# Reordering the first products of a decoder layer, moving one accumulator to other PSUM banks, and giving one chain its own planner clock

## The chip, the cores and the metric

The kernel runs on one core of a Trainium2 chip (trn2). A core has a matrix engine (PE; its weight loads are listed apart as PEld), a vector engine (DVE), an activation engine (ACT), GpSimd (POOL) and a sync engine (SP, which issues most DMAs here). The metric is the device time of one execution in microseconds, the median over several runs. One execution was also taken by the hardware profiler; all rows below are from that one.

## The reference, cut to what matters

Two layers (DEPTH = 2) of a decoder trunk over a sequence of 256 rows of width 1024. In each layer one projection `z = h @ w_in` is split into the inputs of two mixers; their outputs are merged and projected, and an MLP and a gated embedding follow.

```
h = rmsnorm(x, norm_mix[i]);  z = h @ w_in[i]
(q_a, kc, vc, ks_, vs_, kw, vw, g_nsa, rq, rk, rv, rg, merge_a, merge_b) = split_cols(z, IN_SPLITS)
y_a = nsa_mixer(q_a, kc, vc, ks_, vs_, kw, vw, ...) @ w_up_nsa[i]
y_b = retention(rq, rk, rv, rg) @ w_up_ret[i]
mix = sigmoid(merge_a) * y_a + sigmoid(merge_b) * y_b
x = x + mix @ w_out[i]
x = x + square(relu(rmsnorm(x, norm_mlp[i]) @ w_ff1[i])) @ w_ff2[i]
x = x + sigmoid(rmsnorm(x, norm_ple[i]) @ w_ple_gate[i]) * (p[i] @ w_ple[i])
```

In the first mixer the keys and values `kc`, `vc` are cut into overlapping windows of 32 rows, passed through a small MLP (`gelu(zb @ w1) @ w2`) and give 16 compressed keys and values per group; queries attend to those, to the selected blocks and to a sliding window. With 256 rows all blocks are selected.

## The kernel before

**Tiles.** Every matrix product is made from two halves of each operand: `hi`, a copy rounded to the fast matmul type (ACT), and `lo`, the rest (DVE). A product is three matmuls, hi·hi, hi·lo, lo·hi (`three`, L214 records all matmuls). The activations are kept transposed in `XT`, 8 chunks of 128 x 256; their halves, scaled by the norm's gain, are `XH` and `XL` (`feed_x`). The factor of the norm itself comes later: `feed_sq` squares the chunks, `finish_a` sums the squares with one matmul over `ones` and raises to the power -1/2 on POOL (`r`), `finish_b` turns `r` into a row of 256 (`RB`).

**Weights** come in units of 512 KB (128 x 1024; kvg: 280 KB). `PLAN` lists the units in the order in which PE takes them. `unit_load` issues a unit's DMA on SP into one of 4 `raw` buffers, `unit_split` makes `hi` and `lo` into 6 buffers each, `take` hands them to PE, and `advance` keeps the splits 4 units ahead of PE. The first-layer MLP of the compressed keys (`w1`, named w0 to w7) has raw buffers of its own.

**The order on PE** is written out by hand: `ORDER` (L56) for the products from `w_in`, as far as rg3, and `_plan` (L70) for the rest. A kcvc, ksvs, rq or ff1 unit is 24 matmuls of 256 columns, a q, rv or rg unit 12 of 512 columns, a kvg unit 12 of 280, a w unit 4 of 512. `fa` and `fb` call `finish_a` and `finish_b`. `unit` (L863) accumulates q, kvg, ksvs, rv and rg in two banks of the PSUM pool `mm`, which has three; the pool `sc` has two banks and serves the attention's scores, and `ot` one.

**Work beside it.** `windows` (L880) runs when kcvc is complete and `fb` is done: DVE multiplies by `RB` (zt), adds the positions (zs) and splits (ZB), and ZB is what w0 to w7 multiply. `q_tail`, `kv_tail`, `compress`, `attend` (softmax) and `collect` (weigh, retain) are generators: each piece issues its PE, ACT and DVE instructions and yields a time at which the next may come. The planner keeps a virtual clock `vt["pe"]` that each matmul moves on, and books ACT, DVE and POOL work into the free stretches of those engines (`charge`, L157). `poke`, called between groups of matmuls, runs the pieces that are due; so the place of a piece in PE's queue is fixed when the program is built. A tile framework then orders ACT's and DVE's instructions; `tc.high_priority()` moves some ahead.

**At the end of attention**, `weigh` writes NHh and NHl, which the units ua0 to ua3 multiply; among these stand the matmuls (`ot<-rV,rs`) and the transposes of `retain`, whose RHh and RHl the units ub0 to ub3 multiply. In the MLP, `ff1(i)` makes one of 16 groups of 256 hidden columns from two units of four chunks each.

Of the kernel before, what the change touches and what calls it, by code (L numbers as in the profile page):

```python
# [15 lines left out]
P = 128  # L16
S = 256
# [28 lines left out]
for _n, _w in PAR_PARTS:  # L46
# [7 lines left out]


ORDER = (  # L56
# [4 lines left out]
)  # L61


def _seq(s):
    return [(x, 0) if x in ("fa", "fb") else (x[:-1], int(x[-1])) for x in s.split()]


SEQ = [_seq(s) for s in ORDER]


def _plan(l):
    r = [({"w": "w1"}.get(n, n), u) for n, u in SEQ[l] if n not in ("fa", "fb")]
    for n in ("ma", "mb"):
        r += [(n, u) for u in range(8)]
    r += [("ua", u) for u in range(4)] + [("ub", 0), ("ub", 1), ("ub", 2), ("out", 0), ("out", 1)]
    r += [("ub", 3)] + [("out", u) for u in range(2, 8)]
    r += [("ff1", u) for u in range(4)]
    for i in range(14):
        r += [("ff1", 2 * i + 4), ("ff1", 2 * i + 5), ("ff2", 2 * i), ("ff2", 2 * i + 1)]
    r += [("ff2", u) for u in range(28, 32)]  # L80
    r += [("ple", u) for u in range(2)]
    r += [("gate", u) for u in (0, 2, 4, 1, 3, 5, 6, 7)]
    return [(l,) + x for x in r]
# [11 lines left out]
def trunk(ctx: ExitStack, tc: tile.TileContext, xT, wu, wg, cst, msk, par, pin, out):  # L95
# [25 lines left out]
    def mm_tile(shape):  # L121
        return ps.tile(shape, F32, tag="mm", name=nm("mm"), bufs=3)
# [31 lines left out]

    gaps = {e: [[0.0, 1e9]] for e in ("act", "dve", "pool")}

    def charge(eng, us):  # L157
        us += 0.03
        gs = gaps[eng]
        while len(gs) > 1 and gs[0][1] < vt["pe"] - 6.0:  # L160
            gs.pop(0)
        for i, (a, e) in enumerate(gs):
            s = max(a, cur[0])
            if s + us <= e:
                new = []
# [99 lines left out]
    def load_x(a, b_):  # L265
        nc.sync.dma_start(XT[:, a:b_, :], xT[:, a:b_, :])
# [73 lines left out]
    def begin(st):  # L340

        while state["load"] < RAW:
            unit_load(state["load"])
            state["load"] += 1
            if state["load"] in (2, 3):
                load_x(2 * state["load"], 2 * state["load"] + 2)
        unit_split(0, lambda c: feed_x(st, c, 1))
        state["split"] = 1
        split_to(2 - AHEAD)
        for c in range(4, 8):  # L350
            feed_x(st, c, 1)
# [15 lines left out]
    bg = []  # L367
    LB = 7.0
    SL = 0.0
    DE = 1.0  # L370
    SLACK = {"kv_tail": 4.0, "q_tail": 3.0, "compress": 1.5, "attend": 1.0, "collect": 0.0}

    def spawn(gen, paced=False):
        bg.append([vt["pe"], gen, paced])
# [1 line left out]
    def step(gen):  # L376
        fresh()
        if gen.__name__ == "compress":
            with tc.high_priority():
                d = next(gen)  # L380
        else:
            d = next(gen)
        if d == "now":
            return cur[0]
        return (cur[0] if d is None else d) + SLACK.get(gen.__name__, SL)

# [45 lines left out]
    def feed_sq(st, c0, n):  # L432
        sq = ztile([P, n, S])
        act(sq, XT[:, c0:c0 + n, :], AF.Square)
        if c0 == 0:
            st["sq"] = sq
        else:
            acc = st["sq"][:, 0:n]
            tt(out=acc, in0=acc, in1=sq, op=ALU.add)
        if c0 + n == 8:  # L440
            acc = st["sq"]
            tt(out=acc[:, 0], in0=acc[:, 0], in1=acc[:, 1], op=ALU.add)
# [69 lines left out]
    def layer(l, st):  # L512
# [349 lines left out]

        def unit(name, u, k0, nk, width, first, last):  # L863
            if first:
                acc[name] = [mm_tile([P, width]) for _ in range(2)]
            a_unit(acc[name], take(l, name, u), XH, XL, k0, nk, width, first, last)

        def w1_unit(u):
# [45 lines left out]
        for name, u in SEQ[l]:  # L914
            if name == "kcvc":
                b_unit(pkv, take(l, "kcvc", u), XH, XL, 4 * u, u == 0, u == 1)
                if u == 1:
                    ready("kcvc")
            elif name == "fa":
                finish_a(st)  # L920
                r = st["r"]
                rh = small([P, 2], "rh")
                ts(out=rh, in0=r, scalar1=0.5, scalar2=None, op0=ALU.mult)
                rr = small([P, 2], "rr")
                tt(out=rr, in0=r, in1=r, op=ALU.mult)
                ready("fa")
            elif name == "fb":
                finish_b(st)
                RB = st["RB"]
                stt(out=gk, in0=PAR(l, "qn"), scalar=float(DH) ** -0.5, in1=PAR(l, "kn"),  # L930
                    op0=ALU.mult, op1=ALU.mult)
                ready("fb")
            elif name == "kvg":
                unit("kvg", u, 2 * u, 2, 280, u == 0, u == 3)
                if u == 3:
                    ready("kvg")
            elif name == "q":
                unit("q", u, 2 * u, 2, 512, u == 0, u == 3)
                if u == 3:
                    for t in range(2):  # L940
                        spawn(q_tail(t, acc["q"][t]))
                    poke()
            elif name == "ksvs":
                unit("ksvs", u, 4 * u, 4, 256, u == 0, u == 1)
                if u == 1:
                    for t in range(2):
                        spawn(kv_tail(1, t, acc["ksvs"][t]))
                    poke()
            elif name == "w":
                w1_unit(u)  # L950
                if u == 7:
                    spawn(compress(acc["w"]))
                    poke()
                    spawn(attend(), True)
                    spawn(collect(), True)
            else:
                if name in ("rq", "rk"):
                    i, hp = ("rq", "rk").index(name), u // 2
                    if u % 2 == 0:
                        acc[name] = mm_tile([P, 2, S])  # L960
                    b_unit(acc[name], take(l, name, u), XH, XL, 4 * (u % 2), u % 2 == 0, u % 2 == 1)
                    if u % 2 == 1:
                        fresh()
                        rope(i, hp, acc[name])
                    continue
                unit(name, u, 2 * u, 2, 512, u == 0, u == 3)
                if u < 3:
                    continue
                for t in range(2):
                    pq = acc[name][t]  # L970
                    fresh()
                    if name == "rv":
                        act(rV[:, t, :], pq, AF.Copy, scale=rr[:, t:t + 1])
# [85 lines left out]
        act(ph, pT, AF.Copy)  # L1059
        sub(pl, pT, ph.bitcast(F32))  # L1060

        def ff1(i):
            pm = mm_tile([P, 2, S])
            for u in range(2):
                b_unit(pm, take(l, "ff1", 2 * i + u), XH, XL, 4 * u, u == 0, u == 1)
            au = big([P, 2, 2, S], f"B{i % 3}", "au")
            ho = big([P, 2, 2, S], f"B{3 + i % 4}", "ho", F32R)
            a, u2 = au[:, 0], au[:, 1]
            h, o = ho[:, 0], ho[:, 1]
            act(a, pm, AF.Relu)  # L1070
            tt(out=h, in0=a, in1=a, op=ALU.mult)
            act(u2, a, AF.Square)
            sub(o, u2, h.bitcast(F32))
            ff[i] = (h, o)
# [9 lines left out]
                for n in range(4):  # L1084
                    wide(pf[n], w, n, h[:, u, :], o[:, u, :], i == 0 and u == 0, False)

        ff1(0)
        ff1(1)
        finish_a(stf)
        ff1(2)  # L1090
        finish_b(stf, square=True)
# [206 lines left out]
```

## Time and profile before

| | us |
|---|---|
| median of 3 runs | 869.22 (869.02 to 869.53) |
| the profiled execution's own time | 870.81 |
| its span, from the first to the last instruction | 868.70 |
| PE busy | 848.6 (98% of the span) |
| DVE busy | 613.1 (71%) |
| ACT busy | 501.1 (58%) |
| DMA, mean | 175 GB/s |

Rows of the timeline have a start, a duration, the engine and line, what is written from what, and in brackets the idle time just before and what ended it. A matmul's duration is modelled and overlaps the next one's: 0.28 us is listed for one of 256 columns, while 48 of them take 5.70 us, 0.119 each. What a stretch costs on PE is therefore read from starts, and not from busy time.

### The profile page before, as it was taken

The page shows a single profiled execution, that of the slowest core. Times are in us where ns is not written, and L with a number is a line of the kernel's source. Part 1 is how long each engine was busy: PE and PEld are TensorE (multiplying, and loading weights), DVE is VectorE, ACT ScalarE, POOL GpSimd, SP SyncE. Part 2 cuts the span into 40 slices and gives each one's busy share as a digit, 9 for nine tenths or more (in the row PEclk, how much of TensorE's full clock was granted, in tenths as well). Part 3 has the DMA queues.
Part 4 walks back from the last instruction along what each step waited for, and adds up shares of the span by engine and source line. Part 5 has one row for each costly group of instructions (what it writes and reads, how often), then busy time and mean ns, then how long its engine had stood idle before and what let it go on. Part 6 is the DMA issues. An engine that isn't in the chain of part 4 may idle for free.

```text
span 868.7 us, 16475 instructions
## 1 busy us (share of the span) xinstructions
PE 848.6 (98%) x6647; PEld 817.3 (94%) x6647; DVE 613.1 (71%) x1011; ACT 501.1 (58%) x836; POOL 38.9 (4%) x32
## 2 busy tenths in 40 slices
PE   7999999999999999999999999999999999999997
PEld 6799899989999999999998988998999999999997
DVE  6997797867855555556799869886868555555584
ACT  6685876544644444445677759674446444444461
POOL 1130000010000000000013000000000000000000
PEclk9999999999999999999999999999999999999999
DMA  7776444435566666666665653533565656666641
GB/s 246 298 256 214 148 142 133 139 110 173 171 191 185 184 191 180 185 190 218 203 187 166 222 161 114 171 122 112 154 183 176 189 181 185 192 178 187 188 129 49
DMA packets 44284, 152.10 MB, mean 175 GB/s; under 512 B 5169, under 2 KB 6961, under 8 KB 44209
## 3 DMA queue, kind: packets, MB, share of 16 engines
q1 hardware_dynamic: 44064, 151.04, 56.2%
q8 instruction: 52, 0.85, 0.4%
q14 instruction: 24, 0.19, 0.1%
q10 hardware_dynamic: 144, 0.01, 0.0%
HBM read 149.99 MB, written 1.05 MB: 174 GB/s over the span
## 4 chain that ended last, share of the span: by engine, by line
PE 83%; DVE 10%; ACT 2%; issue 2%; DMA 1%; POOL 1%; SPq 0%; DVEq 0%; ACTq 0%; POOLq 0%
PE mm L214 49%; PE sc L214 15%; PE pt L214 13%; PE ot L214 4%; DVE lo L187 3%; PE pt L219 2%; DVE XL L195 1%; ACT hi L183 1%; DVE XT L187 1%; POOL rso L208 1%; DMA raw<-in_wu_dram 1%; DMA XT<-in_xT_dram 1%; DVE zt L187 1%; DVE z L187 1%; DVE tmp L195 0%
## 5 line engine op out<-in xcount | busy, mean ns | idle before, releaser
L187 DVE TENSOR_TENSOR lo<-raw,hi 128x1024 fp32r<-128x1024 f32 (+2 forms) x287 | 342.6, 1197 | 192.4 <-ACT hi L183 191.4
L183 ACT ACTIVATE hi<-raw 128x1024 fp32r<-128x1024 f32 (+2 forms) x287 | 296.2, 1038 | 277.7 <-PE mm L214 167.8
L214 PE MATMUL mm<-XH,hi 128*128 128x256 f32 x992 | 283.4, 286 | 0.0
L214 PE MATMUL mm<-XL,hi 128*128 128x256 f32 x992 | 279.6, 282 | 0.7 <-DVE XL L195 0.7
L214 PE MATMUL mm<-XH,lo 128*128 128x256 f32 x992 | 279.6, 282 | 0.0
L214 PEld LDWEIGHTS mm<-XL,hi 128*128 128x128 f32 x992 | 187.0, 189 | 1.9 <-DVE XL L195 1.1
L214 PEld LDWEIGHTS mm<-XH,hi 128*128 128x128 f32 x992 | 187.1, 189 | 1.2
L214 PEld LDWEIGHTS mm<-XH,lo 128*128 128x128 f32 x992 | 186.9, 188 | 0.0
L214 PE MATMUL sc<-ho,hi 128*128 128x256 f32 x512 | 96.8, 282 | 0.0
L214 PE MATMUL pt<-ho,hi 128*128 128x256 f32 x512 | 96.6, 281 | 0.0
L214 PEld LDWEIGHTS pt<-ho,hi 128*128 128x128 f32 x512 | 78.6, 188 | 0.0
L214 PEld LDWEIGHTS sc<-ho,hi 128*128 128x128 f32 x512 | 78.6, 188 | 0.0
L214 PE MATMUL pt<-ho,lo 128*128 128x256 f32 x256 | 72.0, 281 | 0.0
L214 PE MATMUL sc<-ho,lo 128*128 128x256 f32 x256 | 72.0, 281 | 0.0
L214 PE MATMUL mm<-hi,XH 128*128 128x512 f32 (+2 forms) x160 | 57.7, 361 | 3.8 <-ACT tmp L183 2.6
L214 PE MATMUL mm<-lo,XH 128*128 128x512 f32 (+2 forms) x160 | 56.4, 352 | 0.4 <-DVE lo L187 0.4
L214 PE MATMUL mm<-hi,XL 128*128 128x512 f32 (+2 forms) x160 | 56.4, 353 | 0.0
L214 PEld LDWEIGHTS pt<-ho,lo 128*128 128x128 f32 x256 | 48.2, 188 | 0.0
L214 PEld LDWEIGHTS sc<-ho,lo 128*128 128x128 f32 x256 | 48.2, 188 | 0.0
L208 POOL TENSOR_TENSOR rso<-rsv,mhalf 128x2 f32<-128x2 f32 (+3 forms) x18 | 29.9, 1667 | 295.3 <-DVE rsv L191 295.3
L214 PEld LDWEIGHTS mm<-hi,XH 128*128 128x128 f32 x160 | 30.1, 188 | 8.6 <-ACT tmp L183 3.0
L183 ACT ACTIVATE e<-e,nmx 128x128 f32<-128x128 f32 (+2 forms) x96 | 37.6, 395 | 0.9 <-DVE nmx L203 0.8
(182 smaller groups left out, 1292.9 us busy)
## 6 DMA issues: line engine op xcount, KB each, us to landing
raw<-in_wu_dram SPq DMA_DIRECT2D x275, 512.0 KB, 3.8
raw<-in_wg_dram SPq DMA_DIRECT2D x8, 280.0 KB, 3.7
cst<-in_cst_dram SPq DMA_DIRECT2D x1, 768.0 KB, 7.9
out_dram<-XT SPq DMA_DIRECT2D x3, 256.0 KB, 2.4
XT<-in_xT_dram SPq DMA_DIRECT2D x4, 128.0 KB, 2.9
raw<-in_wu_dram SPq DMA_DIRECT2D x4, 128.0 KB, 3.3
XT<-in_xT_dram SPq DMA_DIRECT2D x2, 256.0 KB, 5.7
tmp<-in_pin_dram SPq DMA_DIRECT2D x2, 256.0 KB, 3.8
```

The source lines that it names most:

```text
L183: return nc.scalar.activation(o, *a, **k)
L187: return nc.vector.tensor_tensor(**k)
L195: return nc.vector.scalar_tensor_tensor(**k)
L208: return nc.gpsimd.tensor_tensor(**k)
L214: return nc.tensor.matmul(o, a, b_, **k)
L219: return nc.tensor.transpose(o, a, i)
```

## The change

It has seven edits:

- `ORDER`: q0 moves ahead of kcvc1, q1 ahead of `fb`, ksvs1 ahead of w0, and each rq unit stands two w units earlier; in the first layer a mark `sq` after q0 is where the squares are summed.
- `begin`: chunks 4 to 7 of XT are loaded behind the first four units instead of among them, and `feed_sq` is no longer called there.
- `unit`: the accumulators of q come from the pool `sc`.
- `charge`: while a piece of `compress` is issued, each of its instructions moves only the chain's own time (its duration, 0.03 and 0.6 us) and books nothing on its engine.
- `SLACK["compress"]` falls from 1.5 to 0.3 and `DE`, by which a score matmul may come ahead of the release of its bank, from 1.0 to 0.5.
- ff1's first two groups are interleaved: unit 0 of both, then unit 1 of both.
- The plan of units follows.

```diff
 ORDER = (
-    "kcvc0 kvg0 kvg1 kcvc1 kvg2 fa kvg3 q0 fb q1 q2 q3 ksvs0 w0 w1 ksvs1 w2 w3 rq0 w4 w5 rq1  "
-    "w6 w7 rq2 rq3 rk0 rk1 rk2 rk3 rv0 rv1 rv2 rv3 rg0 rg1 rg2 rg3",
+    "kcvc0 kvg0 kvg1 q0 sq kcvc1 kvg2 fa kvg3 q1 fb q2 q3 ksvs0 ksvs1 w0 w1 rq0 w2 w3 rq1 w4 w5  "
+    "rq2 w6 w7 rq3 rk0 rk1 rk2 rk3 rv0 rv1 rv2 rv3 rg0 rg1 rg2 rg3",
...
-    r += [("ff1", u) for u in range(4)]
+    r += [("ff1", u) for u in (0, 2, 1, 3)]
...
     def charge(eng, us):
         us += 0.03
+        if first[0]:
+            cur[0] += us + 0.6
+            return
...
-            if state["load"] in (2, 3):
-                load_x(2 * state["load"], 2 * state["load"] + 2)
+        load_x(4, 6)
+        load_x(6, 8)
...
-        for j in range(4):
-            feed_sq(st, 2 * j, 2)
...
-    DE = 1.0
-    SLACK = {"kv_tail": 4.0, "q_tail": 3.0, "compress": 1.5, "attend": 1.0, "collect": 0.0}
+    DE = 0.5
+    SLACK = {"kv_tail": 4.0, "q_tail": 3.0, "compress": 0.3, "attend": 1.0, "collect": 0.0}
...
-                acc[name] = [mm_tile([P, width]) for _ in range(2)]
+                acc[name] = [(s_tile if name == "q" else mm_tile)([P, width]) for _ in range(2)]
...
+            elif name == "sq":
+                for j in range(4):
+                    feed_sq(st, 2 * j, 2)
...
-        ff1(0)
-        ff1(1)
+        ff1_unit(0, 0)
+        ff1_unit(1, 0)
+        ff1_unit(0, 1)
+        ff1_unit(1, 1)
```

**SP at the start of the program.** 128x256 from `in_wu` are quarters of kcvc0, 128x560 are kvg units, 128x1024 the other units, 128x512 of XT two chunks. Before:

```order
L293 DMA raw_113<-in_wg_dram 128x560
L266 DMA XT<-in_xT_dram 128x512
L293 DMA raw_116<-in_wg_dram 128x560
L266 DMA XT<-in_xT_dram 128x512
L302 DMA raw_119<-in_wu_dram 128x1024
L293 DMA raw_187<-in_wg_dram 128x560
```

Now:

```order
L298 DMA raw_113<-in_wg_dram 128x560
L298 DMA raw_115<-in_wg_dram 128x560
L307 DMA raw_117<-in_wu_dram 128x1024
L271 DMA XT<-in_xT_dram 128x512 x2
L307 DMA raw_175<-in_wu_dram 128x1024
L298 DMA raw_177<-in_wg_dram 128x560
```

The unit of 1024 ahead of XT's last chunks is q0; kcvc1 (raw_175) is now the fifth unit, and so the first that needs a raw buffer used before.

**DVE from `fb` to ZB, first layer.** ot is kcvc's accumulator; mm, now sc, are those of q; lo are splits of weight units. Before:

```order
L187 TENSOR_TENSOR zt_176<-ot_185,RB_394 64x2x256
L187 TENSOR_TENSOR lo_376<-raw_264,hi_375 128x1024
L187 TENSOR_TENSOR zt_176<-ot_185,RB_394 64x2x255
L187 TENSOR_TENSOR zt_176<-ot_185,RB_394 64x2x256
L187 TENSOR_TENSOR zt_176<-ot_185,RB_394 64x2x255
L187 TENSOR_TENSOR lo_412<-raw_294,hi_411 128x1024
L187 TENSOR_TENSOR zs_177<-zt_176,cmp 128x16x15 x4
L187 TENSOR_TENSOR V_172<-tmp_349,V_172 128x2x64
L187 TENSOR_TENSOR ZB_178<-zs_177,ZB_178 128x16x32
L187 TENSOR_TENSOR qn_181<-mm_371,qn_181 128x8x64
L187 TENSOR_TENSOR ZB_178<-zs_177,ZB_178 128x16x32
```

Now:

```order
L192 TENSOR_TENSOR zt_164<-ot_173,RB_412 64x2x256
L192 TENSOR_TENSOR zt_164<-ot_173,RB_412 64x2x255
L192 TENSOR_TENSOR zt_164<-ot_173,RB_412 64x2x256
L192 TENSOR_TENSOR zt_164<-ot_173,RB_412 64x2x255
L192 TENSOR_TENSOR lo_430<-raw_314,hi_429 128x1024
L192 TENSOR_TENSOR qn_169<-sc_252,qn_169 128x8x64
L192 TENSOR_TENSOR qn_169<-sc_253,qn_169 128x8x64
L192 TENSOR_TENSOR zs_165<-zt_164,cmp 128x16x15 x4
L192 TENSOR_TENSOR V_160<-tmp_369,V_160 128x2x64
L192 TENSOR_TENSOR lo_453<-raw_316,hi_452 128x1024
L192 TENSOR_TENSOR ZB_166<-zs_165,ZB_166 128x16x32 x2
```

Both subtractions of q (qn), which need q's last matmuls, now stand between zt and zs.

**DVE from the last piece of attention to `retain`, first layer.** PC and o end the last weigh; z and lo_2176 belong to the last mb unit and to a unit of the merge; yss, rsv and tmp normalize retention's output, RHl is its split. Before:

```order
L187 TENSOR_TENSOR o_2112<-ot_1923,o_2112 64x256 x2
L187 TENSOR_TENSOR NHl_175<-o_2112,NHh_174 128x2x128
L195 SCALAR_TENSOR_TENSOR T_1287<-T_1287,mm_2121 128x512
L187 TENSOR_TENSOR lo_2238<-raw_2020,hi_2237 128x1024
L199 TENSOR_REDUCE yss_2155<-tmp_2153 128x4
L191 TENSOR_SCALAR rsv_2157<-yss_2155 128x4
L195 SCALAR_TENSOR_TENSOR tmp_2151<-tmp_2151,rso_2159,rG_184 128x128 x4
L199 TENSOR_REDUCE yss_2204<-tmp_2202 128x4
L195 SCALAR_TENSOR_TENSOR T_1287<-T_1287,mm_2172 128x512
L191 TENSOR_SCALAR rsv_2206<-yss_2204 128x4
```

Now:

```order
L192 TENSOR_TENSOR z_2118<-mm_1999,RB_412 128x512
L192 TENSOR_TENSOR lo_2176<-raw_2000,hi_2175 128x1024
L192 TENSOR_TENSOR o_2109<-ot_1866,o_2109 64x256 x2
L192 TENSOR_TENSOR NHl_163<-o_2109,NHh_162 128x2x128
L200 SCALAR_TENSOR_TENSOR T_1318<-T_1318,mm_2121 128x512
L192 TENSOR_TENSOR lo_2231<-raw_2066,hi_2230 128x1024
L204 TENSOR_REDUCE yss_2155<-tmp_2153 128x4
L196 TENSOR_SCALAR rsv_2157<-yss_2155 128x4
L200 SCALAR_TENSOR_TENSOR tmp_2151<-tmp_2151,rso_2159,rG_172 128x128 x4
L200 SCALAR_TENSOR_TENSOR T_1318<-T_1318,mm_2172 128x512
L192 TENSOR_TENSOR lo_2270<-raw_2122,hi_2269 128x1024
L204 TENSOR_REDUCE yss_2210<-tmp_2208 128x4
```

A z and a lo now stand ahead of o, and a T and a lo ahead of the second yss; on PE the last matmuls of the last mb unit now stand among the last weigh's blocks instead of ahead of them.

## Rows read from the trace of the kernel before

**Rows 1.** The page: the span, and the busy time of each engine.

```profile
span 868.7 us, 16475 instructions
PE 848.6 (98%) x6647; PEld 817.3 (94%) x6647; DVE 613.1 (71%) x1011; ACT 501.1 (58%) x836; POOL 38.9 (4%) x32
```

**Rows 2.** The waits of PE over the whole span: what waited for what, us in total, times, longest.

```profile
PE sc L214 <- DVE nmx L203: 2.0, 4, 0.8
PE mm L214 <- DVE RHl L187: 1.6, 2, 0.8
PE mm L214 <- ACT NHh L183: 1.6, 2, 0.8
PE mm L214 <- DVE XL L195: 0.7, 2, 0.4
```

**Rows 3.** The chain that ended last: a stretch of 48 matmuls of 256 columns and one of 8 of 512 (start, duration).

```profile
57.38 1.86 PE ot L214 x8
...
260.54 5.70 PE mm L214 x48
```

**Rows 4.** PE's timeline at the start: the three gaps after 10 us (in kvg1, twice, and kcvc1).

```profile
12.55 0.39 PE L214 MATMUL mm<-hi,XH 128*128 128x280 f32 x1 [0.73 <-ACT hi L183]
13.37 0.40 PE L214 MATMUL mm<-lo,XH 128*128 128x280 f32 x1 [0.42 <-DVE lo L187]
16.36 0.39 PE L214 MATMUL ot<-XH,lo 128*128 128x256 f32 x1 [1.03 <-DVE lo L187]
```

**Rows 5.** ACT's and DVE's timeline at the start: XH and the squares z of two chunks, hi of kvg1, lo of kvg1, XL of two chunks, a sum of squares, and hi and lo of a whole unit.

```profile
10.51 0.91 ACT L183 ACTIVATE XH<-XT,par 128x256 fp32r<-128x256 f32 x2 [1.27 <-DMA XT<-in_xT_dram]
11.84 0.65 ACT L183 ACTIVATE hi<-raw 128x560 fp32r<-128x560 f32 x1
13.20 0.62 ACT L183 ACTIVATE z<-XT 128x512 f32<-128x512 f32 x1
17.76 1.06 ACT L183 ACTIVATE hi<-raw 128x1024 fp32r<-128x1024 f32 x1 [1.87 <-DMA raw<-in_wu_dram]
...
12.58 0.73 DVE L187 TENSOR_TENSOR lo<-raw,hi 128x560 fp32r<-128x560 f32 x1
13.23 0.87 DVE L195 SCALAR_TENSOR_TENSOR XL<-XT,par,XH 128x256 fp32r<-128x256 f32 x2
14.02 0.68 DVE L187 TENSOR_TENSOR z<-z,z 128x512 f32<-128x512 f32 x1
18.85 1.23 DVE L187 TENSOR_TENSOR lo<-raw,hi 128x1024 fp32r<-128x1024 f32 x1 [1.25 <-ACT hi L183]
```

**Rows 6.** The table of stretches, 20 to 30 us: PE, PEld, DVE, ACT and POOL busy, clock, DMA share, GB/s.

```profile
20.00:30.00 10.00, 9.89 (x55) 8.20 (x54) 7.20 (x18) 8.38 (x16) 2.07 (x3) 1.00 0.99 385
```

**Rows 7.** The timeline around ZB in the first layer: RB (ACT), zt, zs and ZB (DVE), the square of q's first accumulator (ACT), and PE in ksvs0.

```profile
26.41 0.39 ACT L183 ACTIVATE RB<-pt 128x256 f32<-128x256 f32 x1
...
30.20 2.09 DVE L187 TENSOR_TENSOR zt<-ot,RB 64x510 f32<-64x510 f32 x3
...
33.47 2.03 DVE L187 TENSOR_TENSOR zs<-zt,cmp 128x240 f32<-128x240 f32 x4
...
36.94 0.68 DVE L187 TENSOR_TENSOR ZB<-zs,ZB 128x512 fp32r<-128x512 f32 x1
...
37.06 0.69 ACT L183 ACTIVATE tmp<-mm,r 128x512 f32<-128x512 f32 x1 [0.38 <-DVE qn L187]
...
37.80 0.39 PE L214 MATMUL mm<-hi,XH 128*128 128x256 f32 x1 [1.84 <-ACT tmp L183]
```

**Rows 8.** The table of stretches at that gap and just after it (columns as in Rows 6; the sixth value behind the length is the granted clock, as a share of full speed).

```profile
35.70:39.10 3.40, 1.56 (x13) 1.35 (x12) 3.37 (x6) 3.02 (x5) 0.00 (x0) 1.00 0.22 89
39.20:42.50 3.30, 3.30 (x11) 2.62 (x10) 3.30 (x7) 1.96 (x3) 0.46 (x1) 0.50 0.60 186
```

**Rows 9.** PE's timeline in the same stretch of the second layer: the gaps in kcvc1, q0 and ksvs0.

```profile
445.62 0.39 PE L214 MATMUL ot<-XL,hi 128*128 128x256 f32 x1 [0.32 <-DVE XL L195]
...
452.53 0.51 PE L214 MATMUL mm<-hi,XH 128*128 128x512 f32 x1 [0.38 <-ACT gates L183]
...
464.96 0.39 PE L214 MATMUL mm<-hi,XH 128*128 128x256 f32 x1 [0.75 <-ACT tmp L183]
```

**Rows 10.** PE's timeline: the two gaps at score matmuls, first layer.

```profile
94.52 0.48 PE L214 MATMUL sc<-KT,qT 128*128 128x272 f32 x2 [0.21 <-DVE nmx L203]
...
111.74 0.49 PE L214 MATMUL sc<-KT,qT 128*128 128x272 f32 x2 [0.81 <-DVE nmx L203]
```

**Rows 11.** The timeline at the end of attention, first layer: PE's gaps at the last weigh's blocks, at ua0 and at ub0; the copies o (ACT); retention's power on POOL.

```profile
170.72 0.51 PE L214 MATMUL ot<-pp,V 128*128 128x512 f32 x1 [0.22 <-ACT pp L183]
171.58 0.50 PE L214 MATMUL ot<-pp,V 128*128 128x512 f32 x1 [0.35 <-DVE pp L187]
...
172.71 0.77 ACT L183 ACTIVATE o<-ot 64x256 f32<-64x256 f32 x2 [1.57 <-PE ot L214]
...
174.87 0.38 PE L214 MATMUL mm<-NHh,hi 128*128 128x256 f32 x1 [0.78 <-ACT NHh L183]
...
184.49 1.91 POOL L208 TENSOR_TENSOR rso<-rsv,mhalf 128x4 f32<-128x4 f32 x1 [2.52 <-DVE rsv L191]
...
190.56 0.38 PE L214 MATMUL mm<-RHl,hi 128*128 128x256 f32 x1 [0.80 <-DVE RHl L187]
```

**Rows 12.** PE's timeline at the second unit of ff1's first group, first layer.

```profile
229.75 0.39 PE L214 MATMUL mm<-XL,hi 128*128 128x256 f32 x1 [0.33 <-DVE XL L195]
```

More of the change, by code (lines that the diff above doesn't have):

```diff
@@ L56 @@
 ORDER = (
[4 rows of a table removed]
[4 rows of a table added]
 )
 def _seq(s):
-    return [(x, 0) if x in ("fa", "fb") else (x[:-1], int(x[-1])) for x in s.split()]
+    return [(x, 0) if x in ("fa", "fb", "sq") else (x[:-1], int(x[-1])) for x in s.split()]
 SEQ = [_seq(s) for s in ORDER]
 def _plan(l):
-    r = [({"w": "w1"}.get(n, n), u) for n, u in SEQ[l] if n not in ("fa", "fb")]
+    r = [({"w": "w1"}.get(n, n), u) for n, u in SEQ[l] if n not in ("fa", "fb", "sq")]
     for n in ("ma", "mb"):
@@ L155, in trunk @@
     gaps = {e: [[0.0, 1e9]] for e in ("act", "dve", "pool")}
+    first = [False]
     def charge(eng, us):
         us += 0.03
+        if first[0]:
+            cur[0] += us + 0.6
+            return
         gs = gaps[eng]
@@ L378, in step @@
         if gen.__name__ == "compress":
-            with tc.high_priority():
-                d = next(gen)
+            first[0] = True
+            try:
+                with tc.high_priority():
+                    d = next(gen)
+            finally:
+                first[0] = False
         else:
@@ L1060, in layer, with ff1_unit, ff1_end @@
         sub(pl, pT, ph.bitcast(F32))
+        def ff1_unit(i, u):
+            if u == 0:
+                ff[i] = mm_tile([P, 2, S])
+            b_unit(ff[i], take(l, "ff1", 2 * i + u), XH, XL, 4 * u, u == 0, u == 1)
+            if u == 1:
+                ff1_end(i, ff[i])
         def ff1(i):
-            pm = mm_tile([P, 2, S])
             for u in range(2):
-                b_unit(pm, take(l, "ff1", 2 * i + u), XH, XL, 4 * u, u == 0, u == 1)
+                ff1_unit(i, u)
+        def ff1_end(i, pm):
+            fresh()
             au = big([P, 2, 2, S], f"B{i % 3}", "au")
```

4 rows, old and new, of the table ORDER are left out of this document.

## The prediction, made before the changed kernel had run

> **What bounds the kernel.** The page says PE: busy 98% of the span [rows 1]. That hides what can be won, since listed durations overlap; so I read starts. At full pace a matmul of 256 columns starts 5.70 / 48 = 0.119 us after the one before, one of 512 columns 1.86 / 8 = 0.233 [rows 3]. The first matmul after a gap lists 0.39 instead of 0.28, and the 0.28 itself is 0.16 longer than the pace: **a gap costs its idle time and about 0.27 more**. Then I read PE's waits [rows 2] and each gap in its place [rows 4, 7, 9 to 12]. The reader is to see that they stand in four places, twice each: the start of a layer, the first scores, the seam where attention ends and ua0 begins, and ff1's first group. In the middle of the MLP there are none, so nothing there can change.
>
> The sum is made against the profiled execution, 870.81 us (span 868.70 and 2.1 around it). The median of the runs is 1.59 lower; I take the change over to it unchanged.
>
> **Part 1, the start of layer 0.** Before, three gaps after 10 us: 0.73 + 0.42 + 1.03, with 0.27 each 3.0 us [rows 4]. Now kvg1 (280 KB) arrives where two chunks of XT (256 KB) did, whose landing ACT's idle time dates to 10.5 [rows 5]. Its hi takes 0.65 and its lo 0.73, so lo is there at 12.0; kvg0 ends at 11.8 - a gap of about 0.3. kvg1's 12 matmuls end near 13.5. A unit of 512 KB moves in 1.36 us at 385 GB/s [rows 6], so q0 lands at 12.0, hi (1.06) ends at 13.1 and lo (1.23) at 14.4: a gap of 0.7. q0 itself is 12 x 0.233 = 2.8 us, until 17.1. Now kcvc1 needs XT's last four chunks and its own split. On ACT stand four XH (2 x 0.91), two squares (0.62 each) and hi (1.06) behind q0's hi, on DVE four XL (2 x 0.87), two sums (0.68) and lo (1.23) behind q0's lo [rows 5]. ACT: 13.1 + 1.8 + 1.2 + 1.1 = 17.2. DVE: XL end at 16.2, sums at 17.6, lo at 18.8. PE waits from 17.3 to 18.8, 1.5 us. The three new gaps come to 2.5 + 0.8 = 3.3 against 3.0. I take **0**: q0 is more cover, but its bytes and its split stand in front of XT. Ends: -1.4 (one more transfer's time) and +1.5 (kcvc1 split when PE comes).
>
> **Part 2, q's banks and ZB, layer 0.** q's accumulators no longer take two of the three `mm` banks, so ksvs0 need not wait for q's first bank to be squared away: the gap of 1.84, ended by ACT's square of it, goes, 2.1 us [rows 7]. Next late is ZB. Before, RB came at 26.4 and ZB ended at 37.6, 11.2 us later [rows 7], while PE between `fb` and w0 has q2, q3, ksvs0, ksvs1 now, 2 x 2.8 + 2 x 2.86 = 11.3 us (before: q1, q2, q3, ksvs0, the same). By the new order DVE has to end zt (four, 2.8), a lo (1.23), qn (two, which wait for q3), zs (2.03), a lo, ZB. With part 1's times `fb` is at 27.7 and q3 ends at 33.5; qn end near 34.8, zs at 36.9, lo and ZB at 39.7; PE reaches w0 at 39.2. A gap of 0.5 remains, 0.8 with the restart: **+1.3** (ends +0.5 and +2.1).
>
> **Part 3, the clock.** Right after the gap of 1.84 us the granted clock is 0.50, the 1.2 GHz level, for one stretch of 3.4 us (39.2 to 42.6) [rows 8]; it costs half of it, 1.7 us. After no shorter gap, 1.03 at most, does the clock fall. With the gap down to 0.5 I count **+1.7** (ends 0 and 1.7).
>
> **Part 4, the same stretch of layer 1.** Gaps 0.32 + 0.38 + 0.75 and three restarts, 2.3 us [rows 9]. q0 covers kcvc1's last XL by 2.8 us, q's banks need not wait for kvg's release (`gates`), nor ksvs0 for q's. ZB has the same cover of 11.3 us against a chain of about 11; I leave 0.3 for it: **+2.0** (ends +1.3 and +2.3).
>
> **Part 5, scores.** With `DE` 0.5 a score matmul stands about half a microsecond later in PE's queue; the two gaps of a layer, 0.21 + 0.81 + 0.54 = 1.6 us [rows 10], should lose half: +0.8 a layer, **+1.6** (ends -1.1, one more such gap, and +3.1). `compress` itself I cost at nothing: between w7 and the first score stand five to seven units of 2.8 us. Its power on POOL now holds DVE up for some 2 us, since nothing stands between rsv and the product that needs it; behind it wait splits that PE takes four units later.
>
> **Part 6, the seam after attention.** Before, the last weigh's blocks stood in PE's queue with nothing between them: 0.22 + 0.35 + 0.54 = 1.1 us a layer [rows 11]. Now matmuls of the last mb unit separate them: +1.1. But that unit's z and the lo of a unit that only its end lets be split now stand on DVE ahead of o, and on ACT a hi ahead of the copies o: counted from mb's end, z 0.7 and hi 1.06 + lo 1.23 end at 2.5, o (0.9) at 3.4, NHh at 3.8; PE arrives at 1.9 (two matmuls of 512 columns, 12 of 256). A gap of 1.9 instead of 0.78: -1.1. Then retention: its second part is issued 6 matmuls (0.7) later, a hi (1.06) stands ahead of its square, and a lo and RHl ahead of its sum and its rsv; the power takes 1.91 [rows 11]. I get the second transposes some 1.9 us late, where before they were just in time, against 0.6 saved at the first and most of the gap of 0.80 at ub0: -0.9. A layer: 1.1 - 1.1 - 0.9 = -0.9; **-1.8** (ends -4 and +1).
>
> **Part 7, ff1.** Unit 0 of the second group now stands between, 24 matmuls, 2.86 us, ahead of the unit that waited for the last XL: 0.33 and 0.37 [rows 2, 12] and two restarts, **+1.2** (ends +0.6 and +1.2). The cover is 2.86 us for 0.4.
>
> **Part 8, new low clock.** Part 6 makes two gaps of about 1.9 us in each layer, as long as the one that the low clock followed [rows 8]. I count one of the four, **-1.7** (ends -6.8 and 0). The Trainium skill, "TensorE: Matmul & The Clock Gate", its table of advice, names only idle gaps longer than any in this trace as a cause of such a fall; by that rule neither part 3 nor part 8 would count, and the sum would stay as it is, whereas the row applied to all four gaps takes 5.1 more. The trace speaks against the rule at its one gap of 1.84.
>
> **Sum:** 0 + 1.3 + 1.7 + 2.0 + 1.6 - 1.8 + 1.2 - 1.7 = 4.3. 870.8 - 4.3 = 866.5 profiled, **864.9** as a median.
>
> **Rivals.**
> - *The seam costs nothing.* The framework's order on ACT and DVE is looser than my reading, the last blocks are covered, and no low clock follows: parts 6 and 8 become +0.2 and 0. For it: the waits there are all short today [rows 2]. 864.9 - 2.0 - 1.7 = 861.2.
> - *Every long gap brings a low clock.* All four, 5.1 more: 870.0. Against it: two of them need my worst reading of the seam.
> - *The bank was not the wait.* ZB is as late as ksvs0 was: w0 stands for 1.84 us, followed by the low clock. For it: ZB ended 0.1 us before ksvs0 went on [rows 7]. Parts 2 and 3 fall away, 3.0: 867.9, about no change.
> - *Slower: attention starts too early for DVE.* The chain of `compress` books nothing on ACT and DVE, so the planner sets the first scores 1.7 units (4.9 us) earlier against engines that it believes free, and later scores wait as at 111.74, 0.81 + 0.27 = 1.08 each [rows 10]. There are 16 heads with two score products in the two layers. From part 5's gain lost and 5 such waits on it is slower (864.9 + 1.6 + 5.4 = 871.9); with 8 it is 875.1. Against it: the booking is missing for some 2 us only, and well before the scores.
>
> **How the numbers follow.** Forecast 0.47, the seam free 0.20, all low clocks 0.12, ZB late 0.12, slower 0.09. A difference of 0.2% (1.7 us) is about what a measurement of this kernel can tell from no change. The forecast and the free seam are faster, and a part of ZB late; all low clocks is within 0.2% with a share beyond it: faster 0.75, within 0.15, slower 0.10. The range of 8 in 10 runs from the free seam with some of the start's upper end (860.5) to between ZB late and all low clocks (869.3).
>
> **What would show it.** Right: no gap in ksvs0 in either layer and at most 0.5 us ahead of w0; no XL wait in ff1; the full clock from 35 to 46 us; gaps of 1 to 2 us at ua0 and at the second transposes. Wrong: a gap at w0 over 1.5 us, score waits in more than two heads a layer, or a start that reaches q1 later than 25 us. The forecast fails most easily in the seam, since its order on ACT and DVE decides it, and in where the clock falls.

## The result and the profile after

| | before | after |
|---|---|---|
| median, us | 869.14 (868.57 to 869.53, 5 runs) | 865.03 (863.09 to 865.38, 5 runs) |
| the profiled execution, us | 870.81 | 865.38 |
| its span, us | 868.7 | 863.5 |
| ratio | | 0.9948 (95% interval 0.9933 to 0.9962) |

The kernel is 0.5% faster, and the forecast of 864.9 was 0.1 off. That is luck in part: three of the sum's eight terms have the wrong sign, and against the profiled execution, for which it was made, it was 1.1 too high (866.5 against 865.38). Two executions of the kernel before, at 912 and 1100 us with a mean clock of 0.85 and 0.70, are left out of every comparison. The page of the kernel after, its span and busy times, answers to [rows 1]: PE has the same matmuls and the same share; its idle time fell from 20.1 to 18.7 us, and the rest of the gain lies in listed busy time, which counts the restarts behind gaps.

```profile
span 863.5 us, 16468 instructions
PE 844.8 (98%) x6647; PEld 817.0 (95%) x6647; DVE 614.3 (71%) x1011; ACT 500.7 (58%) x836; POOL 37.2 (4%) x32
```

The waits of PE over the whole span after (what waited for what, us in total, times, longest), beside [rows 2]: those for nmx, RHl, XL and for q's bank are gone, the one for NHh has doubled, and those for ZB, KT, tmp and qT are new.

```profile
PE mm L219 <- ACT NHh L188: 3.2, 2, 1.6
PE ot L219 <- DVE ZB L192: 3.2, 2, 1.6
...
PE ot L219 <- DVE lo L192: 1.3, 2, 1.1
PE pt L219 <- DVE KT L200: 1.2, 1, 1.2
PE pt L224 <- DVE tmp L200: 1.0, 2, 0.6
PE pt L224 <- ACT qT L188: 0.7, 1, 0.7
```

What each stretch lost on PE is worked out from the starts: for every matmul the time until the next one starts, less the median of that time for its shape (0.119 us for 256 columns, 0.232 for 512), summed by stretch. The cuts lie at 25, 62, 160 and 200 us in the first layer, at 426, 488.5, 586 and 626 in the second; time at the half clock has a row of its own. (The MLP can be below zero, since medians are subtracted.)

| stretch (part of the forecast) | before | after | gained | forecast |
|---|---|---|---|---|
| start, first layer (1) | 7.5 | 6.1 | 1.4 | 0 |
| fb to w7, first layer (2) | 2.1 | 3.6 | -1.4 | 1.3 |
| the same, with the layer's start, second layer (4) | 2.3 | 3.7 | -1.4 | 2.0 |
| scores, both layers (5) | 4.2 | 1.4 | 2.8 | 1.6 |
| seam, both layers (6) | 9.0 | 7.0 | 2.0 | -1.8 |
| MLP and gate, both layers (7) | 0.6 | -1.2 | 1.8 | 1.2 |
| half clock, at ksvs0 before (3) | 1.5 | 0 | 1.5 | 1.7 |
| half clock, at the second seam after (8) | 0 | 1.5 | -1.5 | -1.7 |
| sum | 27.3 | 22.2 | 5.2 | 4.3 |

PE's timeline at the start after, beside [rows 4]: one gap of kvg1 is left, q0 doesn't wait, and kcvc1 waits as long as it did.

```profile
10.75 0.40 PE L219 MATMUL mm<-lo,XH 128*128 128x280 f32 x1 [0.17 <-DVE lo L192]
18.16 0.39 PE L219 MATMUL ot<-XH,lo 128*128 128x256 f32 x1 [1.06 <-DVE lo L192]
```

The timeline around ZB in the first layer after, beside [rows 7]: `fb` stands on PE at 27.21, but RB follows 1.6 us later, behind the hi of a unit; zt begins when a lo lets it, and qn, zs, one more lo and ZB stand behind each other without a gap. ZB ends 11.7 us after RB; PE had come to w0 at 38.9.

```profile
27.84 1.06 ACT L188 ACTIVATE hi<-raw 128x1024 fp32r<-128x1024 f32 x1
28.79 0.39 ACT L188 ACTIVATE RB<-pt 128x256 f32<-128x256 f32 x1
...
30.62 2.78 DVE L192 TENSOR_TENSOR zt<-ot,RB 64x512 f32<-64x512 f32 x4
...
34.70 1.29 DVE L192 TENSOR_TENSOR qn<-sc,qn 128x512 f32<-128x512 f32 x2
35.90 2.04 DVE L192 TENSOR_TENSOR zs<-zt,cmp 128x240 f32<-128x240 f32 x4
...
38.06 1.21 DVE L192 TENSOR_TENSOR lo<-raw,hi 128x1024 fp32r<-128x1024 f32 x1
39.20 1.28 DVE L192 TENSOR_TENSOR ZB<-zs,ZB 128x512 fp32r<-128x512 f32 x2
...
40.53 0.50 PE L219 MATMUL ot<-hi,ZB 128*128 128x512 f32 x1 [1.60 <-DVE ZB L192]
```

The second layer after, beside [rows 9]: the three small gaps are gone, and two new ones stand there, at w0 and at the first products of `compress`, which wait until KT of `kv_tail` on DVE lets a `pt` bank go. Here `fb` stands at 451.13, and RB 3.0 us behind it.

```profile
454.11 0.39 ACT L188 ACTIVATE RB<-pt 128x256 f32<-128x256 f32 x1
...
463.92 0.68 DVE L192 TENSOR_TENSOR ZB<-zs,ZB 128x512 fp32r<-128x512 f32 x1
...
464.65 0.50 PE L219 MATMUL ot<-hi,ZB 128*128 128x512 f32 x1 [1.63 <-DVE ZB L192]
487.04 0.63 PE L219 MATMUL pt<-cst,tmp 128*128 128x64 f32 x4 [1.19 <-DVE KT L200]
```

The table of stretches after (columns as in [rows 6]; the sixth value behind the length is the granted clock): from 28 to 50 us DVE is busy 21.5 of 22 us. From 39.2 to 42.5, over the gap of 1.60 and just behind it, the clock is full, and behind the gap of 1.62 at the second seam it is half, where [rows 8] had it at ksvs0.

```profile
28.00:50.00 22.00, 19.27 (x122) 16.86 (x121) 21.50 (x39) 17.16 (x29) 9.82 (x6) 1.00 0.78 279
39.20:42.50 3.30, 1.97 (x9) 1.58 (x10) 3.30 (x10) 3.30 (x5) 0.06 (x1) 1.00 0.66 209
596.80:600.10 3.30, 3.30 (x18) 3.30 (x17) 0.31 (x1) 1.21 (x2) 0.00 (x0) 0.50 0.14 56
```

The seam in the first layer after, beside [rows 11]: z and lo stand ahead of o on DVE, so NHh comes late. `retain` has two powers; the 1.91 of [rows 11] is the second, and here the second took 1.01 us.

```profile
168.03 0.69 DVE L192 TENSOR_TENSOR z<-mm,RB 128x512 f32<-128x512 f32 x1 [1.29 <-PE mm L219]
169.00 1.23 DVE L192 TENSOR_TENSOR lo<-raw,hi 128x1024 fp32r<-128x1024 f32 x1 [0.28 <-ACT hi L188]
170.15 0.85 DVE L192 TENSOR_TENSOR o<-ot,o 64x256 f32<-64x256 f32 x2
...
171.03 0.42 ACT L188 ACTIVATE NHh<-o 128x256 fp32r<-128x256 f32 x1 [0.61 <-DVE o L192]
171.50 0.38 PE L219 MATMUL mm<-NHh,hi 128*128 128x256 f32 x1 [1.62 <-ACT NHh L188]
...
182.87 1.01 POOL L213 TENSOR_TENSOR rso<-rsv,mhalf 128x4 f32<-128x4 f32 x1 [4.26 <-DVE rsv L196]
184.40 1.02 PE L224 MATMUL pt<-cst,tmp 128*128 128x128 f32 x4 [0.60 <-DVE tmp L200]
```

### The profile page after: what moved, and what is told of

Read it like the earlier page. It is cut to its first block, busy times and chain, and to the rows that moved or that the text cites. A ratio compares the mean times of both kernels' runs of the same rounds, so it can differ in the third digit from the quotient of the medians.

```text
span 863.5 us, 16468 instructions
## 1 busy us (share of the span) xinstructions
PE 844.8 (98%) x6647; PEld 817.0 (95%) x6647; DVE 614.3 (71%) x1011; ACT 500.7 (58%) x836; POOL 37.2 (4%) x32
## 4 chain that ended last, share of the span: by engine, by line
PE 87%; DVE 7%; ACT 2%; DMA 1%; issue 1%; POOL 1%; SPq 0%; DVEq 0%; ACTq 0%; POOLq 0%
PE mm L219 51%; PE sc L219 16%; PE pt L219 14%; PE ot L219 4%; DVE lo L192 3%; PE pt L224 3%; DMA raw<-in_wu_dram 1%; ACT hi L188 1%; POOL rso L213 1%; DVE zt L192 1%; DVE zs L192 0%; DVE gz L200 0%; DVE XT L192 0%; DVE qn L192 0%; DVE XL L200 0%
## 5 line engine op out<-in xcount | busy, mean ns | idle before, releaser
L219 PE MATMUL mm<-hi,XH 128*128 128x512 f32 (+2 forms) x128 | 44.7, 349 | 0.0
L219 PE MATMUL mm<-lo,XH 128*128 128x512 f32 (+2 forms) x128 | 43.7, 341 | 0.2 <-DVE lo L192 0.2
L219 PE MATMUL mm<-hi,XL 128*128 128x512 f32 (+2 forms) x128 | 43.7, 341 | 0.0
L208 DVE CUSTOM_DVE_ANT_0 e<-sc,masks,nq 128x128 f32<-128x128 f32 (+2 forms) x96 | 29.5, 351 | 1.6 <-PE sc L219 1.0
```

The lines of the kernel that those rows point to most:

```text
L208: return nc.vector.tensor_tensor_reduce(**k)
L219: return nc.tensor.matmul(o, a, b_, **k)
```

## The experiments

Each run was timed beside the kernel before on one chip; ratios are to that. Losses by stretch are worked out as in the table above.

### What removed the score waits, and what placed the last weigh

Four kernels take the planner's edits back, alone or together. **All three:**

```diff
-            first[0] = True
+            first[0] = False
-    DE = 0.5
-    SLACK = {..., "compress": 0.3, ...}
+    DE = 1.0
+    SLACK = {..., "compress": 1.5, ...}
```

> The changed kernel with the three edits of the planner undone: compress books its engines again, SLACK 1.5, DE 1.0; the order of the units, q's banks and ff1 stay. Theory A (the planner's edits removed the score waits, 2.7 us in both layers, and placed the last weigh among the mb unit, 0.7 + 1.2 = 1.9 us, at the price of one stretch of low clock, 1.7): 865.0 + 2.7 + 1.9 - 1.7 = 867.9, score waits of DVE nmx near 1 us in both layers, NHh waits of 0.8 instead of 1.62, no low clock there. Theory B (the new order of units did it, since the rq units stand earlier): 865.0, no score waits, NHh waits of 1.6.

868.25 us, ratio 0.9991 (0.9983 to 1.0). PE's timeline has the score gaps back in both layers, this one the longer of the first:

```profile
110.24 0.49 PE L219 MATMUL sc<-KT,qT 128*128 128x272 f32 x2 [0.84 <-DVE nmx L208]
```

The two layers' seams lose 4.6 each, where the kernel before lost 4.4 and 4.6. Theory A holds, B falls: without the planner's edits all the others together are worth 0.1%, at the edge of what the interval tells. What the planner's edits are worth without the others, on the kernel before, no run shows.

**The clock of `compress` and its SLACK**, DE stays at 0.5 (the first and the last line of the diff above):

> The changed kernel with the clock of compress and its SLACK undone (books its engines, 1.5), DE stays 0.5. If DE took the score waits away: no score waits, the seam as before (NHh 0.8, waits at the last weigh's blocks 0.2 and 0.35), 865.0 + 1.9 - 1.7 = 865.2. If the earlier start of attention took them away: score waits are back, 867.9.

867.89 us, 0.9988 (0.9980 to 0.9997). The time is the second theory's, the mechanism neither's: one score gap of 0.21 a layer is left of the two, so with these other edits DE takes the longer one away, and most of the loss lies in the seam, 5.6 a layer, where a block of the last weigh waits 0.62 and not 0.35.

**DE alone taken back** (1.0):

> The changed kernel with DE at 1.0 again and nothing else. If DE took the score waits away: two score waits a layer come back, 1.35 us with their restarts, 865.0 + 2.7 = 867.7, the seam unchanged. If the earlier start of attention did: 865.0 and no score waits.

866.07 us, 0.9970 (0.9959 to 0.9981). No score wait. So where attention starts early DE adds nothing that these runs can tell, and the second theory holds. This profile has three stretches of half clock.

**The clock alone taken back** (`first[0] = False`, SLACK and DE as changed):

> The changed kernel with compress booking its engines again as before; its SLACK stays 0.3 and DE 0.5. Theory A (the chain's own clock is what sets attention early, so that scores fall where DVE is free and the last weigh among the last mb unit): as in the run with clock and SLACK undone, a score wait a layer, waits at the last weigh's blocks, NHh near 0.77: 867.9. Theory B (SLACK alone, 1.2 us less a piece, is enough): no score waits and 865.4, the seam as in the changed kernel.

867.65 us, 0.9987 (0.9978 to 0.9996). The truth lies between: no score waits, as B had it, and the seam of before, as A had it. PE's timeline at the seam:

```profile
169.18 0.50 PE L219 MATMUL ot<-pp,V 128*128 128x512 f32 x1 [0.36 <-DVE pp L192]
...
172.46 0.38 PE L219 MATMUL mm<-NHh,hi 128*128 128x256 f32 x1 [0.78 <-ACT NHh L188]
```

So the score waits go by the clock with SLACK, and also by SLACK with DE, while of these runs only those with the chain's own clock have the last weigh among mb's last unit. SLACK alone, without either, was not run.

### The seam

The end of the last weigh is drawn ahead of the last six matmuls of mb's last unit (`attended` pokes the pieces until the last weigh is written):

```diff
+            if hold is not None and k == 3:
+                hold()
...
-                    b_unit(pm, take(l, name, 2 * j + u), XH, XL, 4 * u, u == 0, u == 1)
+                    b_unit(pm, take(l, name, 2 * j + u), XH, XL, 4 * u, u == 0, u == 1,
+                           attended if (name, j, u) == ("mb", 3, 1) else None)
```

> The changed kernel with the end of the last weigh drawn ahead of the last six matmuls of mb's last unit instead of behind them, so that o stands ahead of z on DVE and ahead of hi on ACT. Theory A (the gap of 1.62 at ua0 is o's chain behind z, hi and lo; and the half clock in the second layer is a consequence of that gap): the wait for NHh falls to 0.4 at most in both layers and no half clock follows there: 865.0 - 2.4 - 1.7 = 860.9. Theory B (the chain from the last weigh to NHh is as long as it is, whatever stands beside it): the gap falls by less than the 0.7 that PC stands earlier: 864.

**859.55 us**, 0.9890 (0.9877 to 0.9903), better than A expected and the fastest of all. In DVE's and ACT's timeline o now stands ahead of z, and NHh comes at 169.57 instead of 171.03:

```profile
168.62 0.86 DVE L192 TENSOR_TENSOR o<-ot,o 64x256 f32<-64x256 f32 x2 [1.84 <-ACT o L188]
169.51 0.69 DVE L192 TENSOR_TENSOR z<-mm,RB 128x512 f32<-128x512 f32 x1
...
169.57 0.40 ACT L188 ACTIVATE NHh<-o 128x256 fp32r<-128x256 f32 x1
```

PE has no wait for NHh, the seams lose 1.1 each instead of 3.5, and no half clock stands in the span while PE works. Besides the two gaps the wait for `retain`'s tmp went (0.60), though both its powers took longer (1.85 and 1.91 against 1.01); its first part is issued earlier, which I take to be the reason. A wait of 0.35 at RHl came. B falls.

### Where the gain of q's banks went

**q's banks alone, on the kernel before:**

```diff
-                acc[name] = [mm_tile([P, width]) for _ in range(2)]
+                acc[name] = [(s_tile if name == "q" else mm_tile)([P, width]) for _ in range(2)]
```

> The kernel before with q's accumulators in the pool sc and nothing else. Theory A (the gap of 1.84 at ksvs0, and in the second layer those of 0.38 at q0 and 0.75 at ksvs0, are waits for a bank): they go, ZB is there when PE comes to w0 (37.6 against 38.6), and with the half clock 2.1 + 1.7 + 1.7: 869.1 - 3.8 = 865.3 to 863.6. Theory B (ZB was as late as the bank): w0 stands for 1 to 2 us in the first layer and 1 in the second, 868 to 869.

868.12 us, 0.9996 (0.9987 to 1.0006): no difference that can be told. PE's timeline shows both theories at work: the gaps at ksvs0 are gone, but a lo ends a wait of 0.32 at w0 in the first layer and ZB one of 1.14 in the second. From fb to w7 the layers lose 2.2 and 2.0, where it was 2.1 and 2.3; of the profile's loss in this stretch only the half clock went.

```profile
39.72 0.50 PE L214 MATMUL ot<-lo,ZB 128*128 128x512 f32 x1 [0.32 <-DVE lo L187]
...
465.30 0.47 PE L214 MATMUL ot<-hi,ZB 128*128 128x512 f32 x1 [1.14 <-DVE ZB L187]
```

**ZB ahead of q** in the changed kernel:

```diff
-                windows()
+                with tc.high_priority():
+                    windows()
...
-            with tc.high_priority():
-                act(qn[:, :, 0, :].bitcast(F32R), pv, AF.Copy)
+            act(qn[:, :, 0, :].bitcast(F32R), pv, AF.Copy)
```

(and so for q's other two instructions).

> The changed kernel with q's copies, subtractions and squares no longer at high priority and the windows' work (zt, zs, ZB) at high priority, so that on DVE both qn and one lo stand behind ZB instead of ahead of it in the first layer, and one qn in the second. Theory A (the gap of 1.60 at w0 is the order on DVE: qn 1.29 and lo 1.21 ahead of ZB): ZB ends some 2.4 us earlier, at 38.1 where PE comes at 38.9, both gaps of 1.6 with their restarts go, 3.7 us: 861.3; q's transposes wait up to 1 us more: 862.3. Theory B (ZB waits for RB or for ACT's part, and DVE's order only shares the wait out): the gap falls by less than 0.5: 864 to 865.

866.73 us (862.97 to 871.24, 12 runs), 0.9970 (0.9953 to 0.9986). The profiled execution is the slowest of these, 871.24, with four stretches of half clock; the two with a mean clock of 0.999 took 863.0 and 863.1, beside 863.1 and 864.5 of the changed kernel's two at that clock. The timeline of DVE, PE and ACT: ZB ends at 38.1, as A had it, and the first gap is gone, the second down to 0.70. But the second layer waits 3.42 at KT, whose copy stands on ACT behind a hi that waits 3.40 for its load.

```profile
36.82 1.28 DVE L192 TENSOR_TENSOR ZB<-zs,ZB 128x512 fp32r<-128x512 f32 x2
...
465.03 0.50 PE L219 MATMUL ot<-hi,ZB 128*128 128x512 f32 x1 [0.70 <-DVE ZB L192]
...
487.11 1.06 ACT L188 ACTIVATE hi<-raw 128x1024 fp32r<-128x1024 f32 x1 [3.40 <-DMA raw<-in_wu_dram]
...
489.97 1.08 PE L219 MATMUL pt<-cst,tmp 128*128 128x64 f32 x4 [3.42 <-DVE KT L200]
```

From fb to w7 the first layer loses 2.7 instead of 3.6, the second 5.2 instead of 3.7. That the late load, and with it the wait at KT, is as long in the faster executions isn't shown.

**rq0 ahead of w0** (`ksvs0 ksvs1 rq0 w0 w1 w2 w3 rq1`):

> The changed kernel with rq0 ahead of w0 instead of behind w1, in both layers: 24 matmuls, 2.86 us, more between fb and w0. Theory A (w0 waits for a chain of DVE and ACT work that runs from RB to ZB, 11.7 us, and that rq0 does not lengthen): both gaps of 1.6 go with their restarts: 865.0 - 3.7 = 861.3. Theory B (as in the run with ZB first, what is gained at w0 is lost at KT, since the weights' loads behind the w units come late): the wait at KT in the second layer grows from 1.19 to over 2.5: 863.5 to 865.

866.42 us, 0.9976 (0.9962 to 0.9991). No wait for ZB, but PE's timeline has others for the same engine, lo in the first layer and KT in the second; the two stretches lose 3.1 and 3.6. The scores of the first layer lose 1.4 more than in the changed kernel (2.1 against 0.7), with waits of 0.36 for nmx and of 0.58 for an `e` of DVE; that is more than the 0.6 that was saved. Theory B in effect, with the wait at KT smaller than it said; and here too a hi ahead of KT's copy on ACT waits for a load, 1.49 us.

```profile
43.31 0.50 PE L219 MATMUL ot<-lo,ZB 128*128 128x512 f32 x1 [0.72 <-DVE lo L192]
...
488.53 0.63 PE L219 MATMUL pt<-cst,tmp 128*128 128x64 f32 x4 [1.95 <-DVE KT L200]
```

**rq0 first and the seam:**

> Both of the last two edits on the changed kernel. If the two places are independent: 865.0 - 4.1 - 3.7 = 857.2, no wait over 0.7 at w0 and ua0 in either layer, and no half clock after them. If one gap only moves the other or the loads bound the start of attention: 860 to 862.

862.00 us, 0.9914 (0.9898 to 0.9930): slower than the seam alone by the medians, though the ends of the two intervals touch. In PE's timeline KT ends a gap of 3.16, where it was 1.10 with the seam and 1.95 with rq0 first, and on ACT the hi ahead of KT's copy waited 3.14 for its load:

```profile
483.98 1.06 ACT L188 ACTIVATE hi<-raw 128x1024 fp32r<-128x1024 f32 x1 [3.14 <-DMA raw<-in_wu_dram]
...
486.83 0.63 PE L219 MATMUL pt<-cst,tmp 128*128 128x64 f32 x4 [3.16 <-DVE KT L200]
```

**q's low half left out** (ACT writes zeros where DVE subtracted):

```diff
-                sub(qn[:, :, 1, :], pv, qn[:, :, 0, :])
+                act(qn[:, :, 1, :], pv, AF.Copy, scale=0.0)
```

> The changed kernel with q's two subtractions taken from DVE: ACT writes zeros there instead, so that the low half of q is left out. DVE has 1.29 us less in each layer between fb and w0. Theory A (this stretch is bound by DVE's work as a whole, so what is gained at one wait came back at KT in the runs with ZB first and rq0 first): the gap of 1.6 at w0 falls to about 0.3 in both layers and the wait at KT in the second layer does not grow: 865.4 - 2.6 = 862.8. Theory B (ACT, which gets 1.2 us more, or the loads bound it): 864.5 to 866, and w0 still waits over 1 us.

864.68 us, 0.9953 (0.9941 to 0.9966). PE's timeline at w0 in the two layers:

```profile
39.16 0.50 PE L219 MATMUL ot<-hi,ZB 128*128 128x512 f32 x1 [0.37 <-DVE ZB L192]
...
464.94 0.50 PE L219 MATMUL ot<-hi,ZB 128*128 128x512 f32 x1 [1.45 <-DVE ZB L192]
```

In the second layer the wait at KT is gone instead of that at w0. By stretches fb to w7 loses 2.75 and 2.4 instead of 3.6 and 3.7: 2.1 of the 2.6 us taken from DVE came back there, not where A put it. Score waits that the changed kernel doesn't have took 1.3 of it in the second layer. In the median 0.4 to 1.1 us are left, less than the intervals can tell; A is borne out by the stretches and not by the time.

### The start, and the control

**XT's chunks among the first units again:**

```diff
+            if state["load"] in (2, 3):
+                load_x(2 * state["load"], 2 * state["load"] + 2)
-        load_x(4, 6)
-        load_x(6, 8)
```

> The changed kernel with chunks 4 to 7 of XT loaded among the first units again, ahead of kvg1 and ahead of q0; the squares stay behind q0. Theory A (the start is bound by the order of the loads): kvg1 and q0 land 1.0 and 1.2 us later and PE waits for them, kcvc1 still waits for its own lo behind q0's: the start is 1 to 2 us longer, 866.4 to 867.4. Theory B (PE waits for splits, not for loads): XL is there earlier, kcvc1's wait of 1.06 goes, and the start is up to 1 us shorter, 864.4.

866.35 us, 0.9973 (0.9964 to 0.9982). PE waits for kvg1 and q0, as A said, and the half clock lies over the start (PE's timeline, and the table of stretches):

```profile
12.92 0.40 PE L219 MATMUL mm<-hi,XH 128*128 128x280 f32 x1 [1.13 <-ACT hi L188]
...
16.73 0.79 PE L219 MATMUL sc<-lo,XH 128*128 128x512 f32 x1 [0.75 <-DVE lo L192]
```

```profile
15.20:21.90 6.70, 5.95 (x16) 4.38 (x16) 4.21 (x6) 3.17 (x4) 0.00 (x0) 0.50 0.64 192
```

kcvc1's wait is gone too, as B said, but at the half clock PE came later to it. Outside the half clock, in which q0's wait lies, the start loses 6.3, beside the changed kernel's 6.1; and the interval overlaps that of the changed kernel's second measurement below, so a price of the early loads isn't shown in the median.

**The changed kernel once more:**

> The changed kernel unchanged, as the control beside these three on one chip and to see where the half clock falls in another execution. If the half clock is a fixed consequence of the order: one stretch, at the seam of the second layer, and 865.0. If it falls by chance behind gaps of about 1.6 us: the profiled execution shows it at other places or none, and the times spread over about 1.7 or 3.4 us; median 864 to 866.

865.77 us (864.54 to 867.42, 7 runs), 0.9964 (0.9952 to 0.9977). The profiled execution, 864.54, has no half clock while PE works, with the same gaps of 1.62 at both seams. So the order of the instructions does not fix it; what decides it isn't shown.

## Why the prediction was right

**In the total, by terms that cancelled.** Parts 2 and 4 were 6.1 us too high; parts 1, 5, 6 and 7 together 7.0 too low. And nearly all of the gain hangs on the planner's edits of part 5, which I had counted for little: without them 868.25 is left, beside 868.88 for the kernel before.

- **Part 1** took 0 and measured +1.4, near its upper end. The forecast gap of 0.7 at q0 didn't come, and kcvc1 waited 1.06 instead of 1.5. The two profiles with the old order lose 7.5 and 8.0 at the start, the others 5.1 to 6.6 (half clock aside), the one with XT early 6.3 among them; so it isn't shown that moving those loads brought the gain, nor which other edit did.
- **Parts 2 and 4: wrong sign.** That q's bank ended the waits at ksvs0 was right; the run with the banks alone shows it. The step that failed is "ZB at 39.7; PE reaches w0 at 39.2. A gap of 0.5 remains", and its copy in the second layer. The gaps there are 1.60 and 1.63, over the 1.5 that the prediction itself named as a sign of being wrong. I counted the chain from RB and set RB at `fb`, so that in the first layer only q3's end seemed to hold qn back; behind a late zt and a lo, qn ended at 35.99 and not at 34.8. In the trace RB stands on ACT behind `kv_tail`'s copies and one hi, in the second layer two: 1.6 and 3.0 us behind `fb`, where before it was 0.6 (25.80 to 26.41) and 1.2 (454.04 to 455.21). The chain itself, 11.7 and 10.5 us from RB's start to ZB's end, was near the 11 forecast. Behind that lies a limit that I had not looked for: in this stretch of the first layer DVE is busy 21.5 of 22 us (21.9 before), and a part of a wait taken from one place comes back at another. Of the 3.6 us that the first layer loses here, ZB first saved 0.9 and rq0 first 0.5, where the gap with its restart is 1.9. Of the 7.3 of both layers rq0 first saved 0.6 and ZB first, in its slowest execution, cost 0.6 more, while 2.6 us of work taken from DVE saved 2.1. In the second layer DVE (30.6 of 32 us from 456 to 488) isn't the whole cause: there the wait at KT grew behind weights that came late, with ZB first (3.40) and with rq0 first and the seam (3.14). Why those loads were late isn't shown.
- **Part 3: right for the profile, wrong for the median.** The stretch at ksvs0 is gone. But I carried the sum over to the median unchanged, and 1.59 lay between the two because the profiled execution had such a stretch and most have none: of 73 more executions of the kernel before 51 list a mean clock of 0.999 or over, with a median of 868.7, and 17 one of 0.997 or 0.998, with 870.2. The run with q's banks alone bears it out: its profile has no such stretch and its median is that of the kernel before.
- **Part 5: right sign, small, and put down to the wrong edit.** All four gaps went, 2.8 against 1.6. I gave DE the credit; the runs give it to SLACK of `compress` with either its clock or DE. The slower rival (attention too early for DVE) did not occur: no score wait was left.
- **Part 6: wrong sign.** The blocks' gaps went, as said, and NHh's gap is 1.62 against 1.9. What failed is "the second transposes some 1.9 us late ... -0.9": they are 0.60 and 0.40 late, and the gap at ub0 is gone altogether. I counted the second power at the 1.91 of [rows 11], and here it took 1.01, which is 0.9 of the 1.3 in the first layer; the rest I did not trace. That o's chain behind z, hi and lo makes NHh's gap, as part 6 had it, the run with the seam shows.
- **Part 7** was right: no wait for XL is left. By its two gaps 1.2 went; the stretch gained 0.6 more, spread over its matmuls without another gap. No run takes this edit back alone.
- **Part 8** counted one of four long gaps, and one it was, at the second seam, 1.5. That it was one is luck: the second profile of the same kernel has none. Nor does one hold for the median: the kernel's twelve executions list mean clocks from 0.995 to 0.999, where the profile with one stretch lists 0.998 and that without 0.999. The rule of the Trainium skill, "TensorE: Matmul & The Clock Gate", table of advice, by which no gap of 1.62 us would do that, is spoken against by these traces: in the seven profiles that have this gap at ua0, in both layers, the half clock followed 8 of 14.

## What to carry to other kernels

When a wait goes, look at the busy share of the engine that ended it in that stretch alone: where it is 98%, as DVE's from 28 to 50 us, half or more of a wait that two runs took from one place by another order came back in the same stretch. Taking work off that engine gave back more, 2.1 of 2.6 us in the profile. A chain's length is counted from the moment its first link can leave its queue, not from the instruction that feeds it. And a handful of matmuls that need nothing new is worth most just behind the last input of a long chain: six of them held back in each layer took 6.2 us off the median (from 865.77 to 859.55, on one chip).

## What the runs showed of the hardware that was not expected

- The half clock follows the same gap in one execution and not in the next. Of 14 gaps of 1.62 us at ua0 8 were followed by it, of 16 gaps of 1.4 to 2.2 at w0 only 3 (1.83, 1.96 and 2.17), of the two over 3 us at KT both, and none of the NHh gaps of 0.8 in the five profiles that had these. A stretch of 3.4 us cost 1.4 to 1.6 us. The changed kernel's twelve executions lie between 863.1 and 867.4, the four of the seam's version, which has no gap at ua0, between 859.0 and 860.4; four are too few to say that it varies less.
- No single long gap is needed. In the run with ZB first, the clock was half from 11.3 to 14.7 us, with four gaps of 0.25 to 0.61 on PE, the first from 6.9 us on, ahead of it.
- `retain`'s power on POOL (128 x 4) goes with what DVE does beside it. Of the 56 in the fourteen profiles 14 have a `lo` of DVE running beside them and took 1.84 to 1.91 us; 42 have none and took 1.01. In the kernel before it was 1.01 for the first power and 1.91 for the second, in both layers.
